# Half of the last layer's third block of tokens goes from the dense experts to the gathered ones

## The chip, the cores and the metric

The kernel runs on one core of a Trainium2 chip. The core has five engines that work side by side, each through its own list of instructions in order: TensorE (matrix products), VectorE, ScalarE, GpSimd and SyncE, which issues most DMAs. The metric is the device time of one execution in microseconds, lower is better. The kernel before takes 4714.54 us, the median of three runs (4711.78 to 4716.38).

## What is computed

Two layers over 512 latent tokens and 256 context tokens, 1024 channels, all in float32. A layer has attention branches and a merge, which the change does not touch, and then an expert network (PEER): each token picks 16 of 128 x 128 experts in each of 8 heads, 128 slots in all, and adds up their outputs. Cut to what matters:

```python
def peer_ffn(u, wq, subkeys, tab_u, tab_v):            # u: tokens x 1024; tab_u, tab_v: 16384 x 1024
    def block(xb):                                     # 128 tokens
        q = (xb @ wq).reshape(PEER_BLOCK, PEER_HEADS, 2, PEER_DQ)
        s = jnp.einsum('thpk,hpnk->thpn', q, subkeys)
        sv, si = lax.top_k(s, PEER_TOPK)               # 16 of 128, for each half of the key
        ...                                            # 16 x 16 candidates
        fv, fi = lax.top_k(cand, PEER_TOPK)            # 16 of 256
        e = jnp.take_along_axis(cidx, fi, axis=-1)
        gate = jax.nn.softmax(fv, axis=-1)
        act = jax.nn.gelu(jnp.einsum('thkd,td->thk', tab_u[e], xb))
        return jnp.einsum('thk,thkd->td', gate * act, tab_v[e])

for l in range(DEPTH):                                 # DEPTH = 2
    ...                                                # attention branches and their merge -> h, hc
    u2 = h * (1 + mod[:, 4]) + mod[:, 3]
    y2 = peer_ffn(u2, peer_wq[l], peer_subkeys[l], peer_u[l], peer_v[l])
    h = layer_norm(DEEPNORM_ALPHA * h + mod[:, 5] * y2, ln_ffn[l])
    ...                                                # context tokens too, but not in the last layer
```

## The kernel before

Tokens go in blocks of 128. The first layer has six blocks (four latent, two context), the last layer four, since its context tokens are not needed. For each block the expert network is computed in one of two ways, and both run at the same time.

Dense (`dense`): all 16384 experts are computed for the block, and a matrix of gates G, zero where a token did not pick the expert, selects. Here the first four blocks of the first layer and the first three of the last are dense. A loop takes 128 experts at a time, 128 turns. A turn loads 128 rows of u and v (`du`, `dv`, 512 KB each), splits each into a high and a low part (`split`: ScalarE writes the high part, VectorE subtracts it), multiplies u with all dense tokens (`act`: 8 chunks x 3 products by `mm3`, the tokens being the moving operand), applies gelu (`ge`), multiplies by the gates (`dw` on VectorE), splits that (`dwh`, `dwl`) and adds the product with v to the sums of each block (`acc`: 2 halves of 512 channels x 3 products per block, the weights of the product being the 128 tokens of the block). The sums stay in PSUM over all 128 turns. The products with u of 21 blocks of experts (first layer) or 26 (last layer) are computed earlier, in plain float32 and in the gaps of the gate stage (`early_pieces`, result `ge` in DRAM); their turns load it.

Gathered (`gather`): for a block of 128 tokens and each of its 128 slots, an indirect DMA that GpSimd issues (`indirect_dma_start`) fetches one row of u per token (`gu`, 512 KB for the 128 partitions), and VectorE multiplies it with the token and sums (line 1679); then gelu and gate; then the same with v: 128 gathers, each added to the block's output `gy` with its weight (line 1694). The last layer gathers its fourth block: 256 gathers. Each gather waits for a product of TensorE (`paced`), so that the gathers keep step with the loop, and for one of five buffers `gu`. How many stand in a turn is `rate` in `dense`: gathers divided by 120 turns less half of the early ones.

Before the experts, the gate stage (`build_gates`) makes G: per token a one-hot row for each half of the key (`ohA`, `ohB`, VectorE and ScalarE) and one float32 product of the two, copied out by ScalarE and stored to DRAM in 2 MB pieces. `chosen` makes the indices and gates of a block on VectorE; for a gathered block of the last layer it runs at the start of the expert stage.

The order of each engine's instructions is set when the program is built: the code says what depends on what, and a scheduler with priorities lays every engine's list. On the chip each engine works through its list in that order.

After the loop `finish_block` closes each block: times the modulation's gate, plus the residual (`hn`, loaded where the gather buffers were), layer normalisation, out. In the last turns the held products are added block by block (`out`, the order of the blocks 0, 1, 2).

Of the kernel before, what the change touches and what calls it, by code (L numbers as in the profile page):

```python
# [9 lines left out]
F = mybir.dt.float32  # L10
# [21 lines left out]
JB = 4  # L32
# [4 lines left out]
ROT = 1  # L37
HFO = 1
HK = 5
# [51 lines left out]
class Body:  # L91
# [269 lines left out]
    def modulate(self, cols, blocks, h_src, uT, tok=None, pool=None, c0=0, keep=None, ks=range(KC)):  # L361
# [5 lines left out]
        for k in ks:  # L367
# [17 lines left out]
            if tok and blocks[0] in tok:  # L385
                late = lambda k=k, u=u: self.to_tokens(blocks, k, u, tok)
        if late:
            late()

    def to_tokens(self, blocks, k, u, tok):  # L390
        ps = self.ps.tile([128, 512], F, name="mm")
        self.transposes(ps, [u[:, q * 128:(q + 1) * 128] for q in range(len(blocks))])
        for q, b in enumerate(blocks):
            self.nc.scalar.copy(tok[b][:, k * 128:(k + 1) * 128], ps[:, q * 128:(q + 1) * 128])


    def layer(self, l):
# [5 lines left out]
        nd = LB if need else LB - 1  # L403
        dense, sparse = blocks[:nd], blocks[nd:]
        with ExitStack() as st:
            s_ps = ExitStack()
# [31 lines left out]
            kp = self.pool(st, "gk")  # L438
            G = self.dram.tile([128 // JB, 128, nd * 128, JB], F, name=f"G{l}")
            uT = [kd.tile([128, KC, SEQ], R, name=f"u2T{i}") for i in range(2)]  # L440
            with ExitStack() as s2:
# [3 lines left out]
                top = self.peer_front(l, blocks, dense, sparse, uT, uf, kp, tp, hp)  # L445
                self.ge = self.dram.tile([EARLY[l], 128, nd * 128], F, name=f"ge{l}")
                bp = self.pool(s2, "pb", 2)
                self.first_u(l, tp)

                fill = [self.early_pieces(l, i, uf, tp) for i in range(EARLY[l])]  # L450
                if need:
                    k = len(fill)
                    left = range(4 * OC[0] // 16, 4)
                    for i, g in enumerate(left):
                        fill.insert(FIRST + (i + 1) * (k - FIRST) // len(left) + i, self.mod_pieces(l + 1, g, bp, 4, MQ))
                total, steps, done = 8 * len(fill), 128 // GT * nd, UP[l][0]
                fill = self.ahead([x for f in fill for x in f])
# [860 lines left out]
    def peer_front(self, l, blocks, dense, sparse, uT, uf, kp, tp, hp):  # L1318
# [3 lines left out]
        n = 128 * nb  # L1322
        self.x2 = {b: kp.tile([128, D], F, name=f"px{b}") for b in sparse}
        sv = tp.tile([128, NB, 16, 16], F, name="sv", bufs=1)
# [60 lines left out]
    def chosen(self, l, top, b, p, e=None, gt=None, sT=None):  # L1385
# [48 lines left out]
        for x, af in enumerate((av, bv)):  # L1434
# [17 lines left out]
            ij.append(o)  # L1452
        if sT is None:
# [8 lines left out]

    def build_gates(self, n, sT, G, p, bd, last):

        nc = self.nc
        iota = self.iota[:, None, :].to_broadcast([128, GT, 128])
        for t0 in range(0, 128, TG):
            gs = p.tile([128, 128 // JB, TG, JB], F, name="gsb")
            for q in range(0, TG, GT):
# [17 lines left out]
                yield  # L1487
            ends = (0, 1, 128 // JB) if last and t0 + TG == 128 else (0, 128 // JB)
            for a, z in zip(ends, ends[1:]):
# [32 lines left out]
    def dense(self, l, dense, sparse, uT, G, aps, kd, dp, st, late):  # L1522
# [3 lines left out]
        nd = len(dense)  # L1526
        nt = nd * 128
        rest = nd > 3
        rate = len(sparse) * 256 / (GR[l] - ER * EARLY[l])
        acc = []  # L1530
# [66 lines left out]
        for j in range(128):  # L1597
# [20 lines left out]
            if j == 128 - TAIL - 2:  # L1618
# [7 lines left out]
                with tc.issue_after(self.last.ins):  # L1626
# [7 lines left out]
                    for b in sparse + dense:  # L1634
                        self.h[b] = self.hn.tile([128, D], F, name=f"hn{b}")
                        nc.sync.dma_start(self.h[b], self.hd[l, 'mid'][b])
                for b in sparse:
                    finish(b, self.y[b])

        if rest:  # L1640
            out4(js)
            finish(dense[3], [y4[:, h] for h in half])
        for n in range(3):
            if HFO:
                for hf in range(2):
                    for j in js:
                        out(j, n, (hf,))
            else:
# [22 lines left out]
    def gather(self, l, b, x, e, gt, ys):  # L1671
        nc, I, p = self.nc, self.I, self.gp
        act = p.tile([128, 128], F, name="act")
        for k in range(128):
            t = p.tile([128, D], F, name="gu", bufs=5)
# [4 lines left out]
            yield 1  # L1680
        w = p.tile([128, 128], F, name="gwt")
# [3 lines left out]
        ys[b] = [y[:, :512], y[:, 512:]]  # L1685
        for k in range(128):
            t = p.tile([128, D], F, name="gu", bufs=5)
# [127 lines left out]
```

## Time and profile before

| | |
|---|---|
| median of three runs | 4714.54 us |
| the profiled execution | 4709.66 us, its span 4707.9 us |
| busy share of the span | TensorE 96%, VectorE 80%, ScalarE 44%, GpSimd 23% |
| the chain that ended last | 68% TensorE, 10% VectorE, 8% issue, 7% DMA, 5% ScalarE, 2% GpSimd |
| indirect DMAs (GpSimd) | 768, of 402.70 MB; all DMA 1120.38 MB, mean 238 GB/s |
| first layer's expert stage | about 1372 to 2640 us |
| last layer's gate stage | about 3500 to 3712 us |
| last layer's expert stage | 3712 to about 4694 us |

A profile is one execution; its span runs from the first to the last instruction. "Busy" counts instructions in flight; products on TensorE overlap, so their distance from start to start tells what one costs, and not the duration of a record. L and a number is a line of the kernel; helpers such as the three products of `mm3` have the same lines (115 to 117) wherever they are called, and the names, written as result<-operands, tell them apart.

### The profile page before, as it was taken

How to read it: one execution, taken by the hardware profiler on the slowest of the kernel's cores; microseconds unless marked ns; L12 is line 12 of the kernel's file. 1: busy time of each engine (PE TensorE's matmuls, PEld its weight loads, DVE VectorE, ACT ScalarE, POOL GpSimd, SP SyncE). 2: the span in 40 equal slices, each digit the busy share in tenths (PEclk: the TensorE clock that was granted, in tenths of full speed). 3: DMA queues.
4: the chain of work that ended last, by engine and by line, in shares of the span. 5: the costliest groups of instructions: out<-in, count | busy, mean ns of one | idle time of the engine just before them, and what ended most of it. 6: DMA issues, size and time to landing. Idle time of an engine off the chain costs nothing.

```text
span 4707.9 us, 67345 instructions
## 1 busy us (share of the span) xinstructions
PE 4500.2 (96%) x24113; PEld 3811.4 (81%) x24113; DVE 3785.4 (80%) x7649; ACT 2057.3 (44%) x3956; POOL 1073.9 (23%) x772
## 2 busy tenths in 40 slices
PE   7999999999999999999999798898999999999998
PEld 6978888885668888888888697687877888888887
DVE  7857655899989999999999875766698787777777
ACT  4357654225952222222222354665339633333333
POOL 0000000000005555656556200000000044333331
PEclk9999999999999999999999899999999999999999
DMA  7844332623679999999999575543426798888885
GB/s 275 292 143 124 108 98 88 211 71 119 193 240 349 344 346 343 339 355 344 341 343 337 205 282 176 176 144 107 148 90 184 252 350 309 299 298 297 303 297 197
DMA packets 495791, 1120.38 MB, mean 238 GB/s; under 512 B 43312, under 2 KB 244832, under 8 KB 486368
## 3 DMA queue, kind: packets, MB, share of 16 engines
q1 hardware_dynamic: 384864, 713.38, 44.7%
q0 software_dynamic: 110592, 402.70, 23.7%
q8 instruction: 190, 3.11, 0.3%
q14 instruction: 145, 1.19, 0.1%
HBM read 975.14 MB, written 140.80 MB: 237 GB/s over the span
## 4 chain that ended last, share of the span: by engine, by line
PE 68%; DVE 10%; issue 8%; DMA 7%; ACT 5%; POOL 2%; SPq 0%; POOLq 0%; DVEq 0%; ACTq 0%
PE acc L117 5%; PE acc L115 5%; PE act L117 4%; PE acc L116 4%; PE act L115 4%; PE act L116 4%; PE mm L115 3%; PE mm L116 3%; PE mm L117 3%; PE mm L1484 3%; PE sg L115 3%; PE sg L116 3%; PE sg L117 3%; DMA gu<-peer_v,pe 3%; PE S L1506 3%
## 5 line engine op out<-in xcount | busy, mean ns | idle before, releaser
L1676 POOL DMA_INDIRECT gu<-peer_u,pe x384 | 526.4, 1371 | 3023.8 <-DMA dv<-peer_v 1390.7
L1688 POOL DMA_INDIRECT gu<-peer_v,pe x384 | 547.2, 1425 | 539.2 <-PE acc L117 242.3
L115 PE MATMUL act<-u2T,duh 128*128 128x512 f32 (+1 forms) x1656 | 603.2, 364 | 11.7 <-ACT duh L109 11.7
L115 PE MATMUL acc<-dvh,dwh 128*128 128x512 f32 x1536 | 599.8, 391 | 12.3 <-ACT dwh L109 12.2
L117 PE MATMUL act<-u2T,dul 128*128 128x512 f32 (+1 forms) x1656 | 603.3, 364 | 0.4 <-DVE dul L110 0.3
L116 PE MATMUL act<-u2T,duh 128*128 128x512 f32 (+1 forms) x1656 | 602.4, 364 | 0.0
L116 PE MATMUL acc<-dvl,dwh 128*128 128x512 f32 x1536 | 599.5, 390 | 0.0
L1694 DVE SCALAR_TENSOR_TENSOR gy<-gu,gwt,gy 128x1024 f32<-128x1024 f32 x381 | 488.7, 1283 | 116.2 <-DMA gu<-peer_v,pe 111.9
L117 PE MATMUL acc<-dvh,dwl 128*128 128x512 f32 x1536 | 546.4, 391 | 1.6 <-DVE dwl L110 1.4
L1679 DVE SCALAR_TENSOR_TENSOR gu<-gu,px 128x1024 f32<-128x1024 f32 x384 | 462.3, 1221 | 88.8 <-DMA gu<-peer_u,pe 85.6
L109 ACT ACTIVATE dwh<-dw 128x512 fp32r<-128x512 f32 (+1 forms) x256 | 148.2, 579 | 816.0 <-DVE dw L1564 800.1
L109 ACT ACTIVATE dvh<-dv 128x1024 fp32r<-128x1024 f32 x256 | 263.6, 1052 | 335.2 <-PE rot L117 211.2
L109 ACT ACTIVATE duh<-du 128x1024 fp32r<-128x1024 f32 x207 | 218.7, 1057 | 327.1 <-PE act L116 251.5
L115 PEld LDWEIGHTS act<-u2T,duh 128*128 128x128 f32 x1656 | 312.2, 189 | 49.7 <-ACT duh L109 12.5
L115 PEld LDWEIGHTS acc<-dvh,dwh 128*128 128x128 f32 x1536 | 288.3, 188 | 74.6 <-ACT dwh L109 17.6
L116 PEld LDWEIGHTS act<-u2T,duh 128*128 128x128 f32 x1656 | 312.1, 188 | 37.1
L117 PEld LDWEIGHTS acc<-dvh,dwl 128*128 128x128 f32 x1536 | 287.4, 188 | 67.1 <-DVE dwl L110 7.6
L117 PEld LDWEIGHTS act<-u2T,dul 128*128 128x128 f32 x1656 | 311.8, 188 | 36.8 <-DVE dul L110 1.8
L116 PEld LDWEIGHTS acc<-dvl,dwh 128*128 128x128 f32 x1536 | 288.3, 188 | 57.3
L110 DVE TENSOR_TENSOR dvl<-dv,dvh 128x1024 fp32r<-128x1024 f32 x256 | 309.1, 1219 | 27.5 <-ACT dvh L109 24.2
L1506 PE MATMUL S<-u,eu 128*128 128x384 f32 (+1 forms) x752 | 310.1, 536 | 2.8 <-DMA eu<-peer_ut 1.6
L1484 PEld LDWEIGHTS mm<-ohB,ohA 128*128 128x128 f32 x1792 | 233.2, 192 | 97.2 <-ACT ohB L1480 48.6
(394 smaller groups left out, 10728.3 us busy)
## 6 DMA issues: line engine op xcount, KB each, us to landing
dv<-peer_v SPq DMA_DIRECT2D x256, 512.0 KB
du<-peer_ut SPq DMA_DIRECT2D x207, 512.0 KB
G<-gsb SPq DMA_DIRECT2D x26, 2048.0 KB
wmodc<-wmodc SPq DMA_DIRECT2D x84, 512.0 KB
gw<-wgb SPq DMA_DIRECT2D x128, 256.0 KB
Gt<-G SPq DMA_DIRECT2D x31, 1024.0 KB
eu<-peer_ut SPq DMA_DIRECT2D x49, 512.0 KB
Gt<-G SPq DMA_DIRECT2D x31, 768.0 KB
```

The lines of the kernel that those rows point to most:

```text
L109: a = self.nc.scalar.activation(hi, src, AF.Copy)
L110: return a, self.nc.vector.tensor_tensor(lo, src, hi, op=OP.subtract)
L115: mm(out, lh, rh, start=first, stop=False)
L116: mm(out, lh, rl, start=False, stop=False)
L117: self.pe = mm(out, ll, rh, start=False, stop=last)
L1484: self.last = nc.tensor.matmul(ps[:, s % 4, :], A[:, s, :], B[:, s, :], start=True, stop=True)
L1506: nc.tensor.matmul(ps[:, :n], U[:, k, :], uf[:, k, :], start=k == 0, stop=k == KC - 1)
L1676: dma = nc.gpsimd.indirect_dma_start(out=t, out_offset=None, in_=I['peer_u'], in_offset=bass.IndirectOffsetOnAxis(ap=e[:, k:k + 1], axis=0))
L1679: nc.vector.scalar_tensor_tensor(t, t, 1.0, x, op0=OP.mult, op1=OP.mult, accum_out=act[:, k:k + 1])
L1688: dma = nc.gpsimd.indirect_dma_start(out=t, out_offset=None, in_=I['peer_v'], in_offset=bass.IndirectOffsetOnAxis(ap=e[:, k:k + 1], axis=0))
L1694: nc.vector.scalar_tensor_tensor(y, t, w[:, k:k + 1], y, op0=OP.mult, op1=OP.add)
```

## The change

In the last layer the third block (block 2) becomes half dense. Its first 64 tokens stay in the loop; G, the early results, `act`, `dw` and `dwl` have 320 tokens and no longer 384, and the block's products with v have 64 columns of weights. Its other 64 tokens are gathered. To fill 128 partitions, each token stands on two of them, with half of its slots on each: 64 gathers of u and 64 of v, named h. They come first in the list of gathers, and `rate` counts them. `half_to_tokens` lays out those tokens twice; the index and gate tiles are cut and copied by four small DMAs; at the end the two halves of each token's output are added, and block 2 is put together from the dense half (copied from PSUM by ScalarE) and this one. The held products at the end go in the order 2, 0, 1. The constant HFO, which was 1, is gone with the branch that it switched off.

```diff
+            elif tok and self.half in blocks and k % 4 == 3:
+                late = lambda k=k: self.half_to_tokens(k, keep[:, :, 128 * self.half + 64:128 * self.half + 128], tok['h'])
...
+    def half_to_tokens(self, k, u, x):
+
+        ps = self.ps.tile([128, 512], F, name="mm")
+        self.transposes(ps[:64], [u[:, q, :] for q in range(k - 3, k + 1)])
+        cs = slice((k - 3) * 128, (k + 1) * 128)
+        self.nc.scalar.copy(x[:64, cs], ps[:64])
+        self.nc.sync.dma_start(x[64:, cs], x[:64, cs])
...
+        self.half = None if need else dense[-1]
+        nt = nd * 128 - (0 if need else 64)
...
-            G = self.dram.tile([128 // JB, 128, nd * 128, JB], F, name=f"G{l}")
+            G = self.dram.tile([128 // JB, 128, nt, JB], F, name=f"G{l}")
...
-                fill = [self.early_pieces(l, i, uf, tp) for i in range(EARLY[l])]
+                fill = [self.early_pieces(l, i, uf[:, :, :nt], tp) for i in range(EARLY[l])]
...
-                    self.chosen(l, top, b, tp, sT=sT)
-                    for _ in self.build_gates(n, sT, G, bp, BD[n], n == nd - 1):
+                    own = 128
+                    if b == self.half:
+                        own = 64
+                        e, gt = kp.tile([128, 64], I32, name="peh"), kp.tile([128, 64], F, name="pgh")
+                        ef, gf = tp.tile([128, 128], I32, name="he", bufs=1), tp.tile([128, 128], F, name="hg", bufs=1)
+                        self.chosen(l, top, b, tp, sT=sT, e=ef, gt=gf)
+
+                        for i in range(2):
+                            for x, f in ((e, ef), (gt, gf)):
+                                nc.sync.dma_start(x[64 * i:64 * i + 64], f[64:, 64 * i:64 * i + 64])
+                        self.bg.append(self.gather(l, 'h', self.x2['h'], e, gt, self.y))
+                    else:
+                        self.chosen(l, top, b, tp, sT=sT)
+                    for _ in self.build_gates(n, sT, G, bp, BD[n], n == nd - 1, own):
...
-        rate = len(sparse) * 256 / (GR[l] - ER * EARLY[l])
+        rate = (len(sparse) + (self.half is not None) / 2) * 256 / (GR[l] - ER * EARLY[l])
...
-                self.last = self.mm3(acc[2 * n + hf], part(W, slice(n * 128, (n + 1) * 128)), part(V, half[hf]), j == 0, j == js[-1])
+                e = min(nt, n * 128 + 128)
+                self.last = self.mm3(acc[2 * n + hf][:e - n * 128], part(W, slice(n * 128, e)), part(V, half[hf]), j == 0, j == js[-1])
...
+                if self.half is not None:
+
+                    yh, y = self.gz.tile([128, D], F, name="gyf"), self.y['h']
+                    nc.sync.dma_start(yh[64:], y[:64])
+                    nc.vector.tensor_tensor(yh[64:], yh[64:], y[64:], op=OP.add)
...
-        for n in range(3):
-            if HFO:
-                for hf in range(2):
-                    for j in js:
-                        out(j, n, (hf,))
-            else:
-                for j in js:
-                    out(j, n)
-            finish(dense[n], acc[2 * n:2 * n + 2])
+        for n in range(3) if self.half is None else (2, 0, 1):
+            for hf in range(2):
+                for j in js:
+                    out(j, n, (hf,))
+            y = acc[2 * n:2 * n + 2]
+            if dense[n] == self.half:
+                for hf in range(2):
+                    nc.scalar.activation(yh[:64, half[hf]], y[hf][:64], AF.Copy)
+                y = [yh[:, h] for h in half]
+            finish(dense[n], y)
...
-        act = p.tile([128, 128], F, name="act")
-        for k in range(128):
+        n = e.shape[1]
+        act = p.tile([128, 128], F, name="act")[:, :n]
+        for k in range(n):
```

The lists of instructions show what this moves. The first place is GpSimd's whole list of gathers; `pe` and a number are the indices of a block, `peh` those of the half block. Before:

```order
L1676 DMA gu<-peer_u,pe_14722 128x1024 x128
L1688 DMA gu<-peer_v,pe_14722 128x1024 x128
L1676 DMA gu<-peer_u,pe_14847 128x1024 x128
L1688 DMA gu<-peer_v,pe_14847 128x1024 x128
L1676 DMA gu<-peer_u,pe_35918 128x1024 x128
L1688 DMA gu<-peer_v,pe_35918 128x1024 x128
```

With the change:

```order
L1708 DMA gu<-peer_u,pe_14722 128x1024 x128
L1720 DMA gu<-peer_v,pe_14722 128x1024 x128
L1708 DMA gu<-peer_u,pe_14847 128x1024 x128
L1720 DMA gu<-peer_v,pe_14847 128x1024 x128
L1708 DMA gu<-peer_u,peh 128x1024 x64
L1720 DMA gu<-peer_v,peh 128x1024 x64
L1708 DMA gu<-peer_u,pe_35714 128x1024 x128
L1720 DMA gu<-peer_v,pe_35714 128x1024 x128
```

Two groups of 64 gathers are put in ahead of the last layer's fourth block.

The second place is the end of VectorE's list in the last layer. `gy` with a number is the output of the fourth block, to which each gathered row of v is added; `hn` is a residual, `acc` the sums of a dense block in PSUM, `gyf` block 2 put together. Before, the last two adds and what follows them:

```order
L1694 SCALAR_TENSOR_TENSOR gy_39972<-gu,gwt,gy_39972 128x1024
L110 TENSOR_TENSOR dul<-du,duh 128x1024
L1694 SCALAR_TENSOR_TENSOR gy_39972<-gu,gwt,gy_39972 128x1024
L1564 TENSOR_TENSOR dw<-ge,Gt 128x384
L1658 TENSOR_TENSOR gy_39972<-gy_39972,gate 128x512 x2
L110 TENSOR_TENSOR dvl<-dv,dvh 128x1024
L110 TENSOR_TENSOR dwl<-dw,dwh 128x384
L1659 SCALAR_TENSOR_TENSOR hn_43932<-hn_43932,gy_39972 128x512 x2
L1247 BN_STATS lnst<-hn_43932 128x6 x2
L110 TENSOR_TENSOR dul<-du,duh 128x1024
L1564 TENSOR_TENSOR dw<-ge,Gt 128x384
```

With the change, from the last expert turn's `dwl` (which is the first row here) on:

```order
L109 TENSOR_TENSOR dwl<-dw,dwh 128x320
L1726 SCALAR_TENSOR_TENSOR gy_41303<-gu,gwt,gy_41303 128x1024 x4
L1689 TENSOR_TENSOR acc_35778<-acc_35778,gate 128x512
L1689 TENSOR_TENSOR gyf<-gyf,gate 128x512
L1726 SCALAR_TENSOR_TENSOR gy_41303<-gu,gwt,gy_41303 128x1024
L1689 TENSOR_TENSOR gyf<-gyf,gate 128x512
L1689 TENSOR_TENSOR acc_35779<-acc_35779,gate 128x512
L1726 SCALAR_TENSOR_TENSOR gy_41303<-gu,gwt,gy_41303 128x1024
L1689 TENSOR_TENSOR acc_35780<-acc_35780,gate 128x512
L1689 TENSOR_TENSOR acc_35781<-acc_35781,gate 128x512
L1726 SCALAR_TENSOR_TENSOR gy_41303<-gu,gwt,gy_41303 128x1024 x93
L1689 TENSOR_TENSOR gy_41303<-gy_41303,gate 128x512 x2
```

Before, the last add is followed by eight more `dw` and the closing of the fourth block is mixed with them. Now 99 adds stand behind the last `dwl`: six among the multiplications by the gate, 93 after them, and the closing of all blocks follows.

## Rows read from the trace of the kernel before

**Rows 1.** Stretches: us; busy us (count) of TensorE, weights, VectorE, ScalarE, GpSimd; clock, DMA, GB/s.

```profile
1372.00:2640.00 1268.00, 1259.69 (x5543) 1041.41 (x5544) 1171.04 (x1466) 377.14 (x479) 724.05 (x512) 1.00 0.93 341
3500.00:3712.00 212.00, 206.37 (x1149) 157.98 (x1148) 177.68 (x537) 174.56 (x491) 0.00 (x0) 1.00 0.64 191
3712.00:4640.00 928.00, 908.27 (x4476) 808.85 (x4475) 728.51 (x929) 326.68 (x445) 349.60 (x256) 1.00 0.86 306
```

**Rows 2.** The end by time: start us, duration us; TensorE, then VectorE.

```profile
4694.00 0.39 PE L117 MATMUL acc<-dvh,dwl 128*128 128x512 f32 x1
...
4645.75 1.28 DVE L1694 SCALAR_TENSOR_TENSOR gy<-gu,gwt,gy 128x1024 f32<-128x1024 f32 x1
4646.94 0.84 DVE L1564 TENSOR_TENSOR dw<-ge,Gt 128x384 f32<-128x384 f32 x1
...
4685.13 1.30 DVE L1658 TENSOR_TENSOR acc<-acc,gate 128x512 f32<-128x512 f32 x2 [4.55 <-PE acc L117]
...
4703.30 1.41 DVE L1668 SCALAR_TENSOR_TENSOR aff<-aff,lnrr,lnt 128x512 f32<-128x512 f32 x2
```

**Rows 3.** TensorE by time: first and last of runs of equal products.

```profile
4207.11 0.40 PE L115 MATMUL acc<-dvh,dwh 128*128 128x512 f32 x1
...
4210.98 0.39 PE L117 MATMUL acc<-dvh,dwl 128*128 128x512 f32 x1
...
4213.31 0.33 PE L115 MATMUL act<-u2T,duh 128*128 128x384 f32 x1
...
4215.22 0.33 PE L117 MATMUL act<-u2T,dul 128*128 128x384 f32 x1
...
3329.77 0.28 PE L117 MATMUL mm<-wh,mT 128*128 128x256 f32 x1
...
3332.25 0.28 PE L117 MATMUL mm<-wh,mT 128*128 128x256 f32 x1
```

**Rows 4.** The chain of waits at the end of the last gate stage: start us, length.

```profile
3697.99 1.29 PE S L1506 x4
3699.28 4.46 PE mm L1484 x40
```

**Rows 5.** Groups, gate stage: count, busy us, mean ns, idle before.

```profile
L1484 PE MATMUL mm<-ohB,ohA 128*128 128x128 f32 x768 | 99.3, 277 | 3.6 <-ACT ohB L1480 3.5
```

**Rows 6.** Groups, the last layer's expert stage.

```profile
L1688 POOL DMA_INDIRECT gu<-peer_v,pe x128 | 172.2, 1345 | 290.3 <-PE acc L117 236.5 <-issue 19.2 <-PE act L117 17.3
L1694 DVE SCALAR_TENSOR_TENSOR gy<-gu,gwt,gy 128x1024 f32<-128x1024 f32 x125 | 160.4, 1283 | 88.6 <-DMA gu<-peer_v,pe 87.0 <-DVE dw L1564 0.4
L1679 DVE SCALAR_TENSOR_TENSOR gu<-gu,px 128x1024 f32<-128x1024 f32 x128 | 155.5, 1222 | 66.6 <-DMA gu<-peer_u,pe 63.7 <-issue 2.9
...
L1564 DVE TENSOR_TENSOR dw<-ge,Gt 128x384 f32<-128x384 f32 x120 | 101.0, 842 | 5.9 <-DMA ge<-ge 5.9
L110 DVE TENSOR_TENSOR dwl<-dw,dwh 128x384 fp32r<-128x384 f32 x120 | 66.3, 554 | 13.6 <-ACT dwh L109 13.6
```

**Rows 7.** A crowded stretch of the first layer: VectorE by time.

```profile
2607.37 3.91 DVE L1694 SCALAR_TENSOR_TENSOR gy<-gu,gwt,gy 128x1024 f32<-128x1024 f32 x3
```

**Rows 8.** The same stretch: GpSimd by time.

```profile
2609.76 1.01 POOL L1688 DMA_INDIRECT gu<-peer_v,pe  x1 [0.30 <-issue]
2611.07 1.02 POOL L1688 DMA_INDIRECT gu<-peer_v,pe  x1 [0.30 <-issue]
2612.39 1.36 POOL L1688 DMA_INDIRECT gu<-peer_v,pe  x1 [0.30 <-issue]
2614.05 1.83 POOL L1688 DMA_INDIRECT gu<-peer_v,pe  x1 [0.30 <-issue]
```

**Rows 9.** Six us at the start of the last layer's gathers; columns as in the first group.

```profile
3769.00:3775.00 6.00, 6.00 (x33) 5.56 (x32) 6.00 (x8) 0.58 (x2) 2.85 (x2) 1.00 1.03 412
```

**Rows 10.** TensorE, 2 and 128 columns of weights: durations min/median/max in ns.

```profile
L281 PE MATMUL sg<-wmod,cs x16: 591/592/593, 1350.3 to 1364.2; 128*2 128x512 f32 x16
...
L1506 PE MATMUL S<-u,eu x336: 592/592/1061, 1071.4 to 1348.9; 128*128 128x512 f32 x168
```

More of the change, by code (lines that the diff above doesn't have):

```diff
@@ L37 @@
 ROT = 1
-HFO = 1
 HK = 5
@@ L445, in layer @@
                 top = self.peer_front(l, blocks, dense, sparse, uT, uf, kp, tp, hp)
-                self.ge = self.dram.tile([EARLY[l], 128, nd * 128], F, name=f"ge{l}")
+                self.ge = self.dram.tile([EARLY[l], 128, nt], F, name=f"ge{l}")
                 bp = self.pool(s2, "pb", 2)
                 self.first_u(l, tp)
-                fill = [self.early_pieces(l, i, uf, tp) for i in range(EARLY[l])]
+                fill = [self.early_pieces(l, i, uf[:, :, :nt], tp) for i in range(EARLY[l])]
                 if need:
@@ L455, in layer @@
                         fill.insert(FIRST + (i + 1) * (k - FIRST) // len(left) + i, self.mod_pieces(l + 1, g, bp, 4, MQ))
-                total, steps, done = 8 * len(fill), 128 // GT * nd, UP[l][0]
+                total, steps, done = 8 * len(fill), nt // GT, UP[l][0]
                 fill = self.ahead([x for f in fill for x in f])
@@ L1322, in peer_front @@
         n = 128 * nb
-        self.x2 = {b: kp.tile([128, D], F, name=f"px{b}") for b in sparse}
+        self.x2 = {b: kp.tile([128, D], F, name=f"px{b}") for b in sparse + ['h'] * (self.half is not None)}
         sv = tp.tile([128, NB, 16, 16], F, name="sv", bufs=1)
@@ L1452, in chosen @@
             ij.append(o)
-        if sT is None:
+        if e is not None:
             ef = t
@@ L1456, in chosen @@
             nc.vector.tensor_scalar(e, ef, float(l * 16384), None, op0=OP.add)
-        else:
+        if sT is not None:
             ps = self.ps.tile([128, 4, 128], F, name="mm")
@@ L1461, in chosen, with build_gates @@
             nc.vector.tensor_copy(sT[:, 0:3, :], ps[:, 0:3, :])
-    def build_gates(self, n, sT, G, p, bd, last):
+    def build_gates(self, n, sT, G, p, bd, last, own=128):
         nc = self.nc
         iota = self.iota[:, None, :].to_broadcast([128, GT, 128])
-        for t0 in range(0, 128, TG):
+        for t0 in range(0, own, TG):
             gs = p.tile([128, 128 // JB, TG, JB], F, name="gsb")
@@ L1487, in build_gates @@
                 yield
-            ends = (0, 1, 128 // JB) if last and t0 + TG == 128 else (0, 128 // JB)
+            ends = (0, 1, 128 // JB) if last and t0 + TG == own else (0, 128 // JB)
             for a, z in zip(ends, ends[1:]):
@@ L1526, in dense @@
         nd = len(dense)
-        nt = nd * 128
+        nt = nd * 128 - (0 if self.half is None else 64)
         rest = nd > 3
-        rate = len(sparse) * 256 / (GR[l] - ER * EARLY[l])
+        rate = (len(sparse) + (self.half is not None) / 2) * 256 / (GR[l] - ER * EARLY[l])
         acc = []
@@ L1642, in dense @@
             finish(dense[3], [y4[:, h] for h in half])
-        for n in range(3):
-            if HFO:
-                for hf in range(2):
-                    for j in js:
-                        out(j, n, (hf,))
-            else:
-                for j in js:
-                    out(j, n)
-            finish(dense[n], acc[2 * n:2 * n + 2])
+        for n in range(3) if self.half is None else (2, 0, 1):
[4 more added lines that the diff above has]
+            if dense[n] == self.half:
+                for hf in range(2):
+                    nc.scalar.activation(yh[:64, half[hf]], y[hf][:64], AF.Copy)
+                y = [yh[:, h] for h in half]
+            finish(dense[n], y)
     def finish_block(self, l, b, y, tabs, gate, p, z, act):
@@ L1680, in gather @@
             yield 1
-        w = p.tile([128, 128], F, name="gwt")
+        w = p.tile([128, 128], F, name="gwt")[:, :n]
         nc.scalar.activation(w, act, AF.Gelu_apprx_tanh)
@@ L1684, in gather @@
         y = self.gz.tile([128, D], F, name=f"gy{b}")
-        ys[b] = [y[:, :512], y[:, 512:]]
-        for k in range(128):
+        ys[b] = y if b == 'h' else [y[:, :512], y[:, 512:]]
+        for k in range(n):
             t = p.tile([128, D], F, name="gu", bufs=5)
```

## The prediction

> **What bounds the kernel now.** I read the stretches of the span first [rows 1]. In the last layer's expert stage (3712 to 4640 us) TensorE is busy 908 of 928 us at a granted clock of 1.00, its 2.4 GHz level; VectorE is busy 729 us and the DMA engines 86% of the time at 306 GB/s. In the gate stage before it (3500 to 3712) TensorE is busy 206 of 212 us. So both stages that the change touches follow TensorE. Then I read the end, by time [rows 2]. The last add of a gathered row starts at 4645.75, expert products are formed after it (from 4646.94), and TensorE starts its last product at 4694.00. The gathers are over 48 us before TensorE is, and cost the end nothing. Behind TensorE's end come only the last normalisations: VectorE's last piece ends at 4704.7, and the span at 4707.9.
>
> **Less for TensorE in the expert stage.** The products with u (`act`) stream 320 columns and no longer 384. Start to start, 17 products of 512 columns take 3.87 us (0.228 each), 11 of 384 take 1.91 (0.174), 21 of 256 take 2.48 (0.118) [rows 3]. That is a straight line in the columns, so 320 columns lie midway between the last two, at 0.146: 0.028 less. There are 128 blocks of experts less 26 computed early, 24 products each: 2448 x 0.0277 = 68 us. The products with v (`acc`) of the third block now have 64 columns of weights, but still stream 512; I cost that at nothing (the first rival is about it).
>
> **Less for TensorE in the gate stage.** One token's gates are one float32 matmul, which the trace shows as two records. At the end of the stage 40 records take 4.46 us, 0.1115 each [rows 4]; there are 768 for 384 tokens [rows 5]. So 64 tokens x 2 x 0.1115 = 14.3 us. The early experts' products take 1.29 us for four records, 0.3225 each; by columns 320/384 of it, 0.054 less: 26 x 8 x 2 = 416 records x 0.054 = 22.4 us. Together 36.7. VectorE (178 of 212 us) and ScalarE (175) lose a share of the same gates, so TensorE stays ahead of them. The change adds eight transposes, two copies on ScalarE, two of half a tile by DMA, four small DMAs for the indices and two short VectorE operations; these stand beside the early products, and without that cover they cost a few us. I take 30 us for the stage, with 17 and 37 as ends.
>
> **Does the expert stage still follow TensorE?** In the new order of VectorE, 99 of the 384 adds stand behind the last `dwl` of the loop, so 285 lie inside it, 29 more than the 256 of before. VectorE's work in the stage is 729 + 29 x 1.29 [rows 6] less a sixth of `dw` and `dwl` ((101.0 + 66.3)/6 = 28), 738 us, in 928 - 66 = 862 us: 86%. The bytes are 306 x 928 = 284 MB, plus 29 x 0.524 MB, less 5 MB for the smaller gates: 294 MB, or 341 GB/s. The first layer's expert stage shows just that load beside a TensorE that hardly waits: VectorE 92%, 341 GB/s, TensorE 1260 of 1268 us [rows 1]. So I let TensorE keep its pace, with 4 us for new waits, and its end comes at 4694.4 - 68 - 30 + 4 = 4600 us; ends 4585 (less idle, full gain in the gate stage) and 4630.
>
> **What the change puts behind it.** Those 99 adds are the heart of the sum. VectorE works in order: six of them are mixed with the first multiplications by the gate of the token blocks, and 93 then stand in one row behind the last of these, which waits for TensorE's last product. Nothing else is left for TensorE. Behind the 93 stand the closing operations of all four blocks, so nothing hides them. What does one cost? The add itself: three in a row take 3.91 us, 1.30 each [rows 7]; that is the lower end. Its gather's issue on GpSimd takes 1.345 us on average, and with the 0.30 between issues 1.65 [rows 6]; that is the upper end. The row nearest to the case is the crowded stretch of the first layer, where GpSimd issues back to back and VectorE does little but adds: starts 1.31, 1.32 and 1.66 us apart [rows 8], mean 1.43. The transfer, 524,288 bytes, takes 1.27 us at the 412 GB/s seen where the DMA engines had mostly gathers [rows 9], so it is not the slowest of the three. I take 1.43: 93 x 1.43 = 133 us, from 121 to 153.
>
> Against the 1.43 stands a rule of the Trainium skill (SBUF — State Buffer, section "SBUF: two separate sides"): VectorE and GpSimd share a pair of ports, locked for a whole instruction when a VectorE operation has two inputs in SBUF and the GpSimd operation reads SBUF; the later one waits. An add with two inputs beside a gather that reads its indices would be such a pair, and the two would take turns. The rows above show the issue stretched from 1.01 to 1.83 us beside adds, but also 1.01 and 1.02 beside adds that follow each other without a gap, which is no full exclusion; the second rival prices it.
>
> **The end.** Before, VectorE closes three blocks from 4685.13 to 4704.71, 19.6 us [rows 2]. Four take 26.1, less six multiplications by the gate already done (0.65 each, from the pair of 1.30), 22.2; with 2 us for the last residuals to load, 24 (22 to 27). Then 3.2 us to the end of the span, as before.
>
> **Sum.** 4600 + 0.7 (the last multiplication) + 133 + 24 + 3.2 = 4761 us of span, 53 more than 4707.9. The profiled execution took 4709.66 us, so 4763; the median of the runs, 4714.54, lies 4.9 above it, and I predict 4768 us. All low ends together: 4585 + 0.7 + 121 + 22 + 3.2 = 4732, which is 4739 as a median; all high ends: 4630 + 0.7 + 153 + 27 + 3.2 = 4814, which is 4821.
>
> **Rivals.** First, faster: products with half the weight columns take half the time. The third block has 128 x 2 x 3 = 768 products with v; 0.114 us less each is 87 us, TensorE ends at 4513 and the median is 4681. For it speaks only that no row shows such a shape with these operands. Against it: float32 matmuls of 512 columns have a median of 592 ns with 2 columns of weights and with 128 [rows 10]. The change is not slower only if TensorE ends by 4708 - 3.2 - 22 - 121 - 0.7 = 4561, 133 us earlier than before, and the rows give 98. Chance 0.03.
>
> Second: in the row of 93, add and issue take turns on a shared port. 1.28 + 1.01 = 2.29 us each, 213 us instead of 133: 4848. Chance 0.07, because of [rows 7, 8].
>
> Third: the DMA engines do not give the expert stage 341 GB/s. At the 306 of before, 294 MB take 961 us instead of 862, TensorE ends 99 us later, and the median is 4867. For it: 306 GB/s already went with 86% busy, and the last layer moves more per TensorE time than before. Against it: the first layer's stage. It decides from anything below 341; at 325 it costs 43 us. Chance 0.10.
>
> **Chances and range.** The forecast (a row of gathers in the open, TensorE's end between 4585 and 4630) gets 0.78, the rivals 0.03, 0.07 and 0.10, and 0.02 is left for a gain that just balances the row. A measurement of this kernel tells about 0.2% from no change, some 9 us; the forecast and the last two rivals all lie above that. Slower 0.95, same 0.02, faster 0.03. The forecast's own range is 4739 to 4821; with the turns on the port and half of the DMA case it reaches 4848.
>
> **What would show it.** In the profile of the changed kernel: TensorE's last product near 4600 us and TensorE idle for the last 150 to 170 us; in that time VectorE does one add every 1.3 to 1.65 us, and little else until the closing operations; `act` products 0.146 us apart; the gate stage some 30 us shorter; about 340 GB/s in the expert stage with TensorE busy 97% or more. The prediction is wrong if TensorE ends well away from 4600, if the adds are spread among the expert products so that fewer than 90 are left, or if one takes under 1.25 or over 1.7 us.

## The result, and the profile after

The changed kernel takes 4769.77 us, the median of four runs (4768.17 to 4777.47), beside 4713.16 for the kernel before on the same chip. The ratio is 1.0125, 95% interval 1.0112 to 1.0137: slower by 57 us, 2 us above the forecast. Two terms of the sum were off by some 20 us each, in opposite directions, so the total looks better than its parts. One run of e1 below, of 14942.76 us, was a slow one and is left out of its median.

The stretches of the changed kernel, with the columns of [rows 1]: the gate stage, the expert stage as far as TensorE works, the stretch behind TensorE's last product, and the closing.

```profile
3500.00:3680.00 180.00, 174.98 (x1016) 143.55 (x1014) 155.47 (x491) 150.19 (x425) 0.00 (x0) 1.00 0.64 191
3680.00:4560.00 880.00, 867.62 (x4643) 734.67 (x4643) 742.40 (x1039) 330.42 (x463) 392.27 (x285) 0.99 0.93 338
4580.00:4737.00 157.00, 0.00 (x0) 0.00 (x0) 120.40 (x96) 0.00 (x0) 115.18 (x89) 0.51 0.88 304
4737.00:4766.00 29.00, 0.00 (x0) 0.00 (x0) 22.94 (x47) 0.81 (x4) 0.00 (x0) 0.50 0.38 145
```

Read the third row first: 157 us in which TensorE and ScalarE do nothing, VectorE makes adds and GpSimd issues gathers. That is the row of gathers in the open. The second row answers to the third of [rows 1]: TensorE is busy 98.6% there, at 338 GB/s, close to the 341 that the prediction asked for.

The end by time, start and duration in us, TensorE and then VectorE, as in [rows 2]:

```profile
4579.59 0.39 PE L116 MATMUL acc<-dvh,dwl 128*128 128x512 f32 x1
...
4580.05 1.29 DVE L1689 TENSOR_TENSOR acc<-acc,gate 128x512 f32<-128x512 f32 x2
4581.24 6.56 DVE L1726 SCALAR_TENSOR_TENSOR gy<-gu,gwt,gy 128x1024 f32<-128x1024 f32 x5
...
4736.07 1.28 DVE L1726 SCALAR_TENSOR_TENSOR gy<-gu,gwt,gy 128x1024 f32<-128x1024 f32 x1 [0.27 <-DMA gu<-peer_v,pe]
4737.39 1.29 DVE L1689 TENSOR_TENSOR gy<-gy,gate 128x512 f32<-128x512 f32 x2
4741.13 1.29 DVE L1690 SCALAR_TENSOR_TENSOR hn<-hn,gy 128x512 f32<-128x512 f32 x2 [2.45 <-DMA hn<-hmid]
...
4761.62 1.41 DVE L1699 SCALAR_TENSOR_TENSOR aff<-aff,lnrr,lnt 128x512 f32<-128x512 f32 x2
```

The 93 adds run from 4581.24 to 4737.39: 156.2 us, 1.68 each (133 and 1.43 were forecast). The closing takes 25.6 us to 4763.0, and the span ends at 4766.4.

The products on TensorE, start and duration: `act` with 320 columns, and `acc` with 64 columns of weights.

```profile
3676.57 0.31 PE L115 MATMUL act<-u2T,fuh 128*128 128x320 f32 x1
...
3677.60 0.30 PE L116 MATMUL act<-u2T,ful 128*128 128x320 f32 x1
...
4503.65 0.40 PE L114 MATMUL acc<-dvh,dwh 128*64 128x512 f32 x1
...
4504.34 0.39 PE L114 MATMUL acc<-dvh,dwh 128*64 128x512 f32 x1
```

Seven steps of `act` in 1.03 us are 0.147 each. Three steps of `acc` in 0.69 are 0.23: half the columns of weights save nothing.

What the engines waited for from 3720 to 4560 us of the changed kernel (engine, line, releaser: us in total, times, longest):

```profile
POOL gu L1708 <- DVE gu L1711: 186.8, 79, 8.4
POOL gu L1708 <- PE acc L116: 25.7, 12, 6.4
...
PE acc L114 <- ACT dwh L108: 1.0, 1, 1.0
...
DVE gyh L1726 <- DMA gu<-peer_v,peh: 0.2, 1, 0.2
```

The same view of the kernel before, over the same stretch:

```profile
POOL gu L1688 <- PE acc L117: 198.1, 41, 8.1
POOL gu L1676 <- PE acc L117: 155.3, 37, 8.2
...
DVE gy L1694 <- DMA gu<-peer_v,pe: 73.7, 44, 4.3
DVE gu L1679 <- DMA gu<-peer_u,pe: 63.7, 42, 5.6
POOL gu L1676 <- DVE gu L1679: 17.6, 12, 5.0
...
PE acc L115 <- ACT dwh L109: 12.0, 12, 2.5
```

Before, GpSimd waited 353 us for products of TensorE, the pace that the program gives the gathers; a gather was often late, and VectorE waited for it at its add (73.7 and 63.7 us, for v and u). With three gathers for every two of before the pace hardly binds: GpSimd waits for a buffer, the rows lie ready when VectorE comes to them (0.2 us of waiting), and TensorE waits less too.

### The profile page after: what moved, and what is told of

Read it like the earlier page. It is cut to its first block, busy times and chain, and to the rows that moved or that the text cites. A ratio compares the mean times of both kernels' runs of the same rounds, so it can differ in the third digit from the quotient of the medians.

```text
span 4766.4 us, 67517 instructions
## 1 busy us (share of the span) xinstructions
PE 4396.3 (92%) x23993; PEld 3693.4 (77%) x23993; DVE 3890.2 (82%) x7797; ACT 2025.7 (43%) x3895; POOL 1244.7 (26%) x900
## 4 chain that ended last, share of the span: by engine, by line
PE 76%; DVE 10%; ACT 6%; DMA 5%; issue 2%; POOL 0%; SPq 0%; DVEq 0%; POOLq 0%; ACTq 0%
PE acc L114 7%; PE acc L115 7%; PE acc L116 7%; PE act L116 6%; PE act L114 6%; PE act L115 6%; PE mm L116 3%; PE mm L115 3%; PE mm L114 3%; PE sg L114 3%; DMA gu<-peer_v,pe 3%; PE sg L115 3%; PE sg L116 3%; PE mm L1508 2%; PE mm L123 2%
## 5 line engine op out<-in xcount | busy, mean ns | idle before, releaser
L114 PE MATMUL acc<-dvh,dwh 128*128 128x512 f32 (+1 forms) x1536 | 598.9, 391 | 1.5 <-ACT dwh L108 1.5
L115 PE MATMUL acc<-dvl,dwh 128*128 128x512 f32 (+1 forms) x1536 | 599.7, 391 | 0.0
L114 PE MATMUL act<-u2T,duh 128*128 128x512 f32 (+1 forms) x1656 | 581.9, 351 | 17.0 <-ACT duh L108 17.0
L116 PE MATMUL act<-u2T,dul 128*128 128x512 f32 (+1 forms) x1656 | 581.9, 351 | 0.6 <-DVE dul L109 0.6
L115 PE MATMUL act<-u2T,duh 128*128 128x512 f32 (+1 forms) x1656 | 581.5, 351 | 0.0
L116 PE MATMUL acc<-dvh,dwl 128*128 128x512 f32 (+1 forms) x1536 | 526.8, 390 | 0.0
L1708 POOL DMA_INDIRECT gu<-peer_u,peh x64 | 90.7, 1418 | 1164.5 <-DVE c L1430 1064.8
L115 PEld LDWEIGHTS acc<-dvl,dwh 128*128 128x128 f32 (+1 forms) x1536 | 274.6, 179 | 70.8
L116 PEld LDWEIGHTS acc<-dvh,dwl 128*128 128x128 f32 (+1 forms) x1536 | 273.1, 179 | 71.0
L114 PEld LDWEIGHTS acc<-dvh,dwh 128*128 128x128 f32 (+1 forms) x1536 | 274.4, 179 | 68.2 <-ACT dwh L108 2.0
L1508 PEld LDWEIGHTS mm<-ohB,ohA 128*128 128x128 f32 x1664 | 221.7, 193 | 93.8 <-ACT ohB L1504 51.8
```

What stands on the lines that cost most here:

```text
L114: mm(out, lh, rh, start=first, stop=False)
L115: mm(out, lh, rl, start=False, stop=False)
L116: self.pe = mm(out, ll, rh, start=False, stop=last)
L1508: self.last = nc.tensor.matmul(ps[:, s % 4, :], A[:, s, :], B[:, s, :], start=True, stop=True)
L1708: dma = nc.gpsimd.indirect_dma_start(out=t, out_offset=None, in_=I['peer_u'], in_offset=bass.IndirectOffsetOnAxis(ap=e[:, k:k + 1], axis=0))
```

## The experiments

The first theory: the work fits into the loop, the loss is the row of gathers behind it, and the row goes at the pace of a round through five buffers. The rivals: GpSimd's issues and VectorE's adds hold each other up; the DMA engines set the pace, in the row or in the loop.

**The two halves of the change.** The smaller dense part without the gathers of h (e1):

```diff
-                        self.bg.append(self.gather(l, 'h', self.x2['h'], e, gt, self.y))
...
-        rate = (len(sparse) + (self.half is not None) / 2) * 256 / (GR[l] - ER * EARLY[l])
+        rate = len(sparse) * 256 / (GR[l] - ER * EARLY[l])
```

> The changed kernel with the gathers of h and their adds left out (half of block 2 gets no expert output here; rate is 2.39 again); all of the smaller dense part stays. Theory (the dense side gains about 98 us, and the row of gathers behind TensorE gives it back and 57 us more): TensorE starts its last product at 4580 to 4600 us, the closing of three blocks follows, and the span ends near 4605 (4595 to 4625), some 100 us below the kernel before and some 160 below the changed one. Rival (something other than TensorE, VectorE or the DMA engines, already bounds the loop, so that the dense saving is not worth its 98 us): the span ends at 4640 or later.

Measured: 4604.49 us, ratio 0.9766 (0.9746 to 0.9785). The dense saving is worth 105 us, 7 more than the 98 of the sum. Then the gathers without the saving (e8):

```diff
-        nt = nd * 128 - (0 if need else 64)
+        nt = nd * 128
...
-                        own = 64
```

> The other part of the change alone: h is gathered (its sum is formed and not used), while the dense part keeps all 384 tokens in the gate stage, the early products and the loop. 64 adds stand behind the last dw. Theory: TensorE's end stays where it was in the kernel before, 4690 to 4715, then 58 to 64 adds in a row at 1.69, 98 to 108 us, and the closing, 29: span 4820 to 4850. Rival (the dense part's saving is what the gathers slow down, not the row): the span ends near 4708 + 165 = 4873 or later, with TensorE's end after 4735.

Measured: 4811.27 us in one run, 104 above before, and so somewhat under the theory's range. VectorE and TensorE of this kernel, by time:

```profile
4680.87 0.39 PE L116 MATMUL acc<-dvh,dwl 128*128 128x512 f32 x1
...
4779.44 1.29 DVE L1684 TENSOR_TENSOR gy<-gy,gate 128x512 f32<-128x512 f32 x2
```

TensorE ends 13 us earlier than before, not later, although more goes on beside it: the gathers are no longer late. From there to the closing it takes 98.6 us, nearly all of it the row of adds. The halves add up to 0 (-105 and +104), the change costs 57. The difference is in the row: a loop that is shorter by the dense saving leaves room for fewer adds: 100 stand behind the last `dw` (99 behind the last `dwl`) and not 64, and 36 x 1.68 = 60 us.

From the first `act` product to TensorE's last product the loop takes 985.5 us before, 908.4 in e1, 964.3 in e8 and 903.4 in the changed kernel. The prediction had 68 us of saving; e1 has 77 without one gather more. VectorE waits 55 us for gathered rows there (47.9 for v, 6.8 for u, from 3720 to 4560 us), against 137 before. So more gathers per turn are not needed for most of the recovery; why the rows come in time in e1 is not shown.

**What sets 1.68 us in the row.** Only the number of buffers is changed (seven in e2, shown here, four in e3), with `gy` put where the tokens' copy was, to make room:

```diff
-            t = p.tile([128, D], F, name="gu", bufs=5)
+            t = p.tile([128, D], F, name="gu", bufs=5 if self.need else 7)
...
-        y = self.gz.tile([128, D], F, name=f"gy{b}")
+        y = self.gz.tile([128, D], F, name=f"gy{b}") if self.need else x
```

> Seven buffers gu in the last layer and no longer five (the sums gy take the place of the token copies px to make room). 71 adds then stand behind the last dw, not 100. Theory (the row of adds goes round the buffers: a gather's issue waits for the add of five gathers earlier, and one round takes 8.45 us, so 1.69 per gather): with seven, 8.45/7 = 1.21, less than the add itself, so VectorE sets the step: 1.30 to 1.40 us; the row takes about 95 us and the span ends near 4705. Rival one (GpSimd's issue and VectorE's add hold each other up): 1.65 to 1.70 as before, row 119 us, span near 4730. Rival two (the DMA engines, 88% busy at 304 GB/s in the row): the same 1.65 to 1.70, and 312 GB/s is not passed.

> Four buffers gu in the last layer. 103 adds stand behind the last dw. Theory (round through the buffers): 8.45/4 = 2.11 us per gather in the row, a little less if the transfers get faster with fewer under way; the row takes about 215 us, the span ends near 4825. Rivals (issue against add, or DMA engines): 1.68 us per gather, the span ends near 4782.

Measured: seven buffers 4723.54 us (ratio to before 1.0028, 1.0016 to 1.0040), four buffers 4801.39 in one run. A stretch of the row, columns as in [rows 1], with seven buffers:

```profile
4606.00:4690.00 84.00, 0.00 (x0) 0.00 (x0) 75.81 (x60) 0.00 (x0) 62.12 (x55) 0.52 0.97 353
```

and with four:

```profile
4590.00:4765.00 175.00, 0.00 (x0) 0.00 (x0) 116.73 (x92) 0.00 (x0) 109.17 (x92) 0.50 0.83 271
```

The adds (VectorE's count) are 84/60 = 1.40 us apart with seven buffers and 175/92 = 1.90 with four; five gave 1.68. So with four and five buffers their number sets the step, which neither rival for the row allows. But the round is not the constant that I had put down: 4 x 1.90 = 7.6, 5 x 1.68 = 8.4, 7 x 1.40 = 9.8 us, and both spans miss what the theory expected (4799.6 and not 4825 with four, 4720.2 and not 4705 with seven). With seven the buffers hardly bind: an issue starts 2.44 us after the end of the add that freed its buffer (the median of 51; with five 1.12). GpSimd's issues then follow each other 0.30 us apart with one exception, VectorE is 90% and the DMA engines are 97% busy; which of the three sets the 1.40 is not shown. TensorE also ended 25 us later (4604.6), which the first theory did not foresee. The round can be followed by time in the changed kernel:

```profile
4598.83 1.28 DVE L1726 SCALAR_TENSOR_TENSOR gy<-gu,gwt,gy 128x1024 f32<-128x1024 f32 x1 [0.87 <-DMA gu<-peer_v,pe]
4599.07 1.85 POOL L1720 DMA_INDIRECT gu<-peer_v,pe  x1 [0.30 <-DMA gu<-peer_v,pe]
...
4601.23 1.63 POOL L1720 DMA_INDIRECT gu<-peer_v,pe  x1 [0.30 <-issue]
...
4607.17 1.28 DVE L1726 SCALAR_TENSOR_TENSOR gy<-gu,gwt,gy 128x1024 f32<-128x1024 f32 x1 [0.17 <-DMA gu<-peer_v,pe]
```

The first add ends at 4600.11 and frees its buffer, the issue into it starts at 4601.23, and the add of what it fetched, five adds later, at 4607.17: 8.34 us for five.

The first rival is half right all the same. The issue at 4599.07 starts inside the first add and ends at 4600.92, 0.81 us after it. Of the 89 issues behind TensorE's end, 78 start inside an add, and 77 of them end 0.81 us after it, whether they last 1.02 or 1.97 us; the one that starts in the first 0.1 us of its add, and the 11 that meet none, take 0.94. The adds do not wait in turn: when their rows are there, they follow each other 0.04 us apart. So an issue waits for the running add. The next issue starts 0.30 us behind it, and that makes the 1.12 us from the add's end to the issue into the buffer it freed: this wait is a part of the round.

**Place or work?** The changed kernel with its adds forced into the loop (e4):

```diff
-            nc.vector.tensor_tensor(W, ge, self.Gt[:, :, j % JB], op=OP.mult)
+            op = nc.vector.tensor_tensor(W, ge, self.Gt[:, :, j % JB], op=OP.mult)
+            if not self.need and len(marks) >= 3 and marks[-3]:
+                tc.add_manual_dep(op.ins, self.adds[marks[-3] - 1].name, mybir.DependencyInfo(
+                    mybir.DependencyClass.NoSync, mybir.DependencyReason.DATA), reason="the gathers keep their place in the loop")
```

> The changed kernel with one kind of order edge more: each dw of the loop stands in VectorE's list behind the gather adds that the program put three turns earlier. Then none of the 384 adds stands behind the last dw; work and buffers are the same. Theory (the price is the place of the adds in VectorE's list and not the work): VectorE has 742 + 99 x 1.28 = 869 us in the stage and TensorE 867, so the loop stays near TensorE's pace, ends 0 to 50 us later than 4580, and with the closing the span ends near 4640 (4610 to 4680), below the kernel before. Rival one (the DMA engines carry no more than about 340 GB/s beside the loop): 297 MB + 52 MB take 1025 us, TensorE ends near 4700 and the span near 4730. Rival two (five buffers let one gather pass each 1.9 us or more when the loop runs): 384 x 1.9 = 730 us, which does not bind.

Measured: 4746.66 us, ratio 1.0063 (1.0045 to 1.0082). My theory fell here by 100 us: no row is left in the open, and the loop itself became longer, with TensorE's last product at 4728.52. Rival one had the number. Three more kernels asked whether it had the cause. Each takes e4 and halves something: the adds' columns (e5), the bytes (e6), both (e9). The first two lines are e5's for the product with u, the others e6's for v; `w5` is 512 in the last layer, and e9 keeps one add of e6's two.

```diff
-            op = nc.vector.scalar_tensor_tensor(t, t, 1.0, x, op0=OP.mult, op1=OP.mult, accum_out=act[:, k:k + 1])
+            op = nc.vector.scalar_tensor_tensor(t[:, :w5], t[:, :w5], 1.0, x[:, :w5], op0=OP.mult, op1=OP.mult, accum_out=act[:, k:k + 1])
...
-            dma = nc.gpsimd.indirect_dma_start(out=t, out_offset=None, in_=I['peer_v'],
+            dma = nc.gpsimd.indirect_dma_start(out=t[:, :w5], out_offset=None, in_=I['peer_v'].rearrange('n (h d) -> (n h) d', d=w5),
...
-                op = nc.vector.scalar_tensor_tensor(y, t, w[:, k:k + 1], y, op0=OP.mult, op1=OP.add)
+                for c in range(0, D, w5):
+                    op = nc.vector.scalar_tensor_tensor(y[:, c:c + w5], t[:, :w5], w[:, k:k + 1], y[:, c:c + w5], op0=OP.mult, op1=OP.add)
```

> As e4, all adds forced into the loop, but in the last layer each gather add works on 512 of the 1024 channels (the other half of the gathered output is left out); the transfers are whole. VectorE loses 384 x (1.28 - 0.65) = 242 us in the stage. Theory (the DMA engines bound e4's loop: 354 MB at 341 GB/s, 94% busy): nothing is gained, the span ends at 4744 +- 15, and the stage still moves 340 to 350 GB/s. Rival (VectorE, with its order written out, bounds e4's loop): the loop returns to TensorE's pace, span 4620 to 4650.

> As e4, but in the last layer each gather fetches 512 channels (half a row of the table, seen as twice as many rows), and two adds of 512 columns use them, so VectorE keeps its work and 101 MB less are moved (what is fetched is not what the reference wants). Theory (DMA engines): 253 MB in the stage leave the engines free, the loop follows TensorE and VectorE (890 us of work), TensorE starts its last product at 4590 to 4640 and the span ends at 4605 to 4660. Rival (VectorE's order): span stays near 4744. Rival (number of packets and not bytes): the packets are as many as before, the span stays near 4744 as well, at half the GB/s with the DMA engines over 90% busy.

> As e6 (half a row per gather), and with one add of 512 columns instead of two, so that VectorE is relieved as well (what is fetched and added is not what the reference wants). Theory (e4's loop was bound by the DMA engines, and e6's, at 260 GB/s, by VectorE, busy 848 of 900 us): with both gone TensorE sets the pace, waits under 25 us in the loop, starts its last product near 4590 (4580 to 4605), and the span ends at 4595 to 4625. Rival (the order edges themselves, or GpSimd's 384 issues, hold the loop): the span stays above 4660.

Measured, in one run each: 4739.95, 4687.03 and 4612.32 us. The spans of e5 (4738.2) and e9 (4610.5) lie in the theory's ranges; e6's, 4685.3, lies 25 us above its range and 59 below its rivals. The stretch from 3700 to 4560 us, columns as in [rows 1], of the kernel with everything whole (e4):

```profile
3700.00:4560.00 860.00, 766.91 (x3952) 632.24 (x3951) 741.36 (x999) 276.69 (x391) 457.14 (x334) 0.98 0.95 347
```

with half the adds (e5):

```profile
3700.00:4560.00 860.00, 770.27 (x3941) 637.00 (x3939) 567.82 (x978) 275.58 (x387) 371.16 (x335) 0.97 0.94 347
```

with half the bytes (e6):

```profile
3700.00:4560.00 860.00, 805.34 (x4186) 664.82 (x4185) 809.96 (x1579) 287.29 (x409) 507.53 (x355) 0.98 0.76 260
```

and with half of both (e9):

```profile
3700.00:4560.00 860.00, 848.36 (x4520) 710.53 (x4518) 664.24 (x1118) 313.33 (x446) 465.01 (x384) 1.00 0.82 283
```

The third number, VectorE's busy time, falls from 741 to 568 us in e5, and TensorE gains nothing. With fewer bytes TensorE goes from 767 to 805, where VectorE, at 810 of 860 us, is next; with both relieved it is back at 848, although GpSimd issues all 384 gathers. So in e4 the transfers bind first and VectorE stands close behind. That it is the engines' rate fits the 347 GB/s at a DMA share of 0.94 to 0.95, which e4, e5 and e12 below share with different adds, gathers and buffers. The waits do not name a DMA: TensorE waits for `dwh` (91.3 us in this stretch from 3720 on), and a late transfer shows only as a buffer that comes free late. So a part could still be the round through five buffers; e4's order with seven wasn't run.

**Fewer tokens.** If the loop has room up to 347 GB/s, half as many gathered tokens should pay. Here 32 tokens are gathered, each on four partitions, and dense keeps 352, cut from the edit:

```diff
-        nt = nd * 128 - (0 if need else 64)
+        nt = nd * 128 - (0 if need else 32)
...
-                        own = 64
+                        own = 96
...
-        rate = (len(sparse) + (self.half is not None) / 2) * 256 / (GR[l] - ER * EARLY[l])
+        rate = (len(sparse) + (self.half is not None) / 4) * 256 / (GR[l] - ER * EARLY[l])
```

It ran in four forms: with e4's order edges (e7), without them (e10), with edges two turns looser (`marks[-5]`, e11), and without edges but with seven buffers, which leave no add behind the loop (e12).

> Only the last 32 tokens of block 2 are gathered, each on four partitions with 32 of its slots (32 gathers of u and 32 of v), dense has 352 tokens; adds forced into the loop as in e4. Theory (a threshold: the loop can take gathers until the DMA engines carry about 347 GB/s): the stage moves half of the additional bytes, 291 + 31 = 322 MB, 928 us at 347 GB/s, and TensorE wants 986 - 33 = 953, so it stays the bound; the gate stage gains 16 us; TensorE starts its last product at 4645 to 4665 and the span ends at 4660 to 4685, 25 to 45 us below the kernel before. Rival (each gather put into the loop has its price, as e4 against e1: 142 us for 128): 4655 + 64 x 1.1 = 4726, above the kernel before.

> As e7 (32 tokens gathered), without the order edges: 22 adds stand behind the last dw. Theory: TensorE ends a little earlier than in e7 (4674.8), at 4655 to 4670, since fewer adds stand in its way; then 22 less the few that are mixed with the gate multiplications, 18 x 1.69 = 30 us, and the closing, 29: span 4710 to 4730, 20 to 40 us above e7. Rival (in the list or behind it is the same): the span ends within 8 us of e7's 4689.6.

> As e7, with each dw behind the adds of five turns earlier and no longer three. Theory (what TensorE still waits in e7, some 30 us for dwh, is VectorE waiting at an add for a transfer that is late): with two turns more the adds come when their rows are there, TensorE waits 10 to 20 us less and the span ends at 4668 to 4682. Rival (the DMA engines at 342 GB/s are the wait itself): within 5 us of 4689.6.

> As e10 (32 tokens gathered, no order edges), with seven buffers gu; by that alone none of the 320 adds stands behind the last dw. Theory (the bytes decide: about 322 MB have to pass in the stage; e7 and e10 pass them at 335 to 342 GB/s on average, and seven buffers reached 348 in e2): 322/0.347 = 928 us from 3697, so TensorE's last product starts at 4630 to 4655, the closing takes 16, and the span ends at 4650 to 4675, 10 to 40 us below e7 and e10. Rival (e7's 38 us of waits come from adds in VectorE's list that stand ahead of dw, and seven buffers only bunch them): the span ends at 4680 to 4695 as e7, e10 and e11.

| kernel | median, us | ratio to before (95%) | TensorE's last product | span, us |
|---|---|---|---|---|
| e7, edges | 4688.59 | 0.9953 (0.9941 to 0.9965) | 4674.81 | 4689.6 |
| e10, no edges | 4688.61 | 0.9950 (0.9931 to 0.9968) | 4628.24 | 4683.9 |
| e11, looser edges | 4686.40 | 0.9943 (0.9930 to 0.9956) | 4674.62 | 4689.1 |
| e12, no edges, seven buffers | 4671.66 | 0.9905 (0.9890 to 0.9920) | 4652.22 | 4669.9 |

All four beat both kernels; e12 is 42 us faster than the kernel before. e7 came out near the threshold theory, 5 us above its range, and far from the 4726 of a fixed price per gather. e10 was a miss: I gave it 4710 to 4730, and its rival, within 8 us of e7, held. e11 missed too (4668 to 4682), and its rival held. e12 came out within its range. The stretch from 3700 to 4560 us in e7:

```profile
3700.00:4560.00 860.00, 827.82 (x4217) 714.77 (x4216) 735.45 (x985) 304.41 (x420) 395.70 (x295) 1.00 0.94 342
```

in e10:

```profile
3700.00:4560.00 860.00, 856.30 (x4390) 746.82 (x4391) 733.45 (x975) 321.25 (x440) 387.75 (x280) 1.00 0.93 339
```

and in e12:

```profile
3700.00:4560.00 860.00, 844.31 (x4319) 733.94 (x4318) 740.08 (x981) 310.34 (x429) 416.16 (x298) 1.00 0.95 347
```

Left alone, TensorE hardly waits in e10 (856 of 860 us) and ends 47 us before e7's, 9 of which it has at its first `act` product; the row of 22 adds and the longer closing give that back. The edges keep 15 gathers more in the stretch and cost TensorE 28 us there. This is not VectorE standing at an add whose row is late: two turns more change nothing in e11, and in e7 VectorE waits for no gathered row at all from 3720 to 4560 us. Only e12 puts more through the DMA engines in the same time, and gains.

## Why the prediction was right or wrong

- **TensorE's savings: right.** `act` at 0.147 (0.146 forecast); the gate stage brought the first `act` product from 3708.45 to 3676.18, 32 us (30 forecast).
- **"4 us for new waits": wrong, in sign.** TensorE ended at 4580, under the range of 4585 to 4630. From the first to the last product the loop became 82 us shorter, 68 of which were forecast. The step assumed that more gathers bring more waiting. In fact the kernel before waited for gathers that its pace made late; e8, with the same gathers beside the full dense part, shows the same recovery (TensorE's end at 4680.87, before 4694.00). But e1, with no gather more, has 77 of the 82, so what makes the gathers come in time there stays open.
- **The 93 adds in one row behind TensorE: right** in place and number.
- **"I take 1.43": mis-sized.** 1.68 us each, 156 us and not 133, just over my upper end of 153. I took the step of four issues in the first layer and weighed add, issue and transfer singly. The row is a round: a gather may not start before the add five gathers earlier has ended, and e2 and e3 show the step move with the number of buffers. Four issues, as in [rows 8], were too few to show such a step. That the total came out within 2 us is luck: TensorE's end, 20 us early, offsets the 23 us of this term.
- **The closing: right.** 25.6 us within 22 to 27, with the wait for the residuals at 2.45.
- **First rival (half the columns of weights, half the time): refuted** by 0.23 us per product.
- **Second rival (add and issue take turns, 2.29 us): refuted in its price, half right in its mechanism.** With seven buffers 60 adds take 1.40 each, which turns would not allow. But an issue that starts inside an add ends 0.81 us after it (77 of 78), while the adds go on 0.04 us apart. The Trainium skill (SBUF — State Buffer, "SBUF: two separate sides") has whichever starts first hold the shared ports for its whole instruction; the trace agrees for the add that comes first, and not for the issue that comes first. [rows 7, 8] had it already: the three adds end at 2611.28, and the issue at 2611.07 ends at 2612.09, 0.81 later.
- **Third rival (the stage does not get 341 GB/s): did not come, but was close.** The stage ran at 338 with TensorE 98.6% busy. Ask for more and it comes: e4's loop stays at 347. The Trainium skill (DMA: Bandwidth & Descriptors, "Where 436 GB/s comes from") gives about 358 GB/s as the limit of a core's transfers from HBM; the long stretches here, 347 and 353 GB/s, agree, the 412 of [rows 9] does not, for 6 us. I should have drawn the budget: from 3676 to 4740 the changed kernel moves 352 MB (1064 us at 331 GB/s; e4 355, 1040 us at 341), which at 347 GB/s takes 1014 to 1023 us, against the 903 of TensorE's loop. With the 16 us from TensorE's last product to the end in e4 the span would end at 4706 to 4715 wherever the gathers stand, by this estimate no better than the 4707.9 of before. The place of the adds, on which my first theory put the blame, is worth only about the 23 us between the changed kernel and e4.

## What to carry to other kernels

Work moved from a busy engine to transfers has to fit the bytes of the stage: add them up against the highest rate that a long stretch of the trace has kept (here 347 GB/s), and choose the share at which both ends meet; half the share turned a loss of 57 us into a gain of 19 to 27 with five buffers (e7, e10, e11) and of 42 with seven (e12). A row of dependent fetch-and-use steps costs its round divided by the number of buffers (1.90 us with four, 1.68 with five), not the longest of its parts, until something else is slower (1.40 with seven). And what an engine gains from a forced order has to be weighed against what the forcing costs the engine that it shares buffers and queues with: e7 and e10 came out equal.

## What the runs showed of the hardware

- Transfers of 512 KB under load take longer well before the engines are full: `dv`, from issue to landing, has a median of 4.5 us at a DMA share of 0.82 (e9, whose gathers are half as large), 5.8 at 0.91 (e1), 6.5 at 0.93 (the changed kernel) and 6.8 at 0.95 (e4).
- Half-size rows (e9) move 283 GB/s at a share of 0.82, which is 345 at a share of 1; e4's whole rows move 347 at 0.95, which is 365. So the busy engines moved some 5% less with half-size rows in the gathers.
- In the row of the changed kernel an issue that starts inside an add ends 0.81 us after it (77 of 78) and lasts from 1.02 to 1.97 us by that; one that meets no add takes 0.94. The next issue starts 0.30 us later, 1.12 us after the end of the add that freed its buffer (the median). What holds the issue was not tried.
